# Values of the last two heads as a half slab behind the last queries and keys, and one plain loop of steps and products after it

## The chip, the cores and the metric

The kernel runs on one core of one Trainium2 chip. The metric is the device time of one execution in microseconds. In the text PE is TensorE, DVE is VectorE, ACT is ScalarE, POOL is GpSimd and SP is SyncE, as in the profile.

## The reference

Two decoder layers over 512 tokens of width 1024: a causal convolution module first, then differential attention; each is followed by a SwiGLU network and a gated input embedding. The change lies in the attention layer:

```
u = rms_norm(h, attn_norm_g)
q, k, v = split(u @ w_qkv)                    # 8 heads; each has two query/key halves of 64 and a value of 128
q, k = rms_norm per half
probs = softmax(q k^T + bias, causal)          # per head and half, in blocks of 128 queries
o = (probs[half 0] - lam * probs[half 1]) @ v
h = h + (rms_norm(o) * const) @ w_o
```

## The kernel before

Every large product is made as three products of TensorE (`mm3`, lines 162 to 166): each operand is split into a high and a low part, and low*high, high*low and high*high are added up in one PSUM bank. Weights come in tiles of 128x1024 through `weight` (lines 147 to 160): one DMA on SP's queue, a copy on ACT (L157, the high part) and a subtraction (L159, the low part) on VectorE, or on GpSimd where the caller asks for it. Raw tiles have two buffers, the split ones four.

**Queries, keys and values.** The table `QKV` (line 89) lists six slabs of w_qkv in order: queries and keys of a pair of heads ("q", 0 to 3) or values of four heads ("v", 0 and 1). A slab is 512 columns wide and takes four weight tiles (`slab`). For each of four blocks of 128 tokens, `tokens` multiplies eight chunks of the activations (stationary, 128x128) with the slab's columns (moving, 512 wide): 24 products. A value block is evicted by ACT (L867, high) and VectorE (L868, low) into the tile of that block. A query/key block is copied and squared by ACT (L884, L887), summed by VectorE (L891), its root is taken by GpSimd (L223) and applied by GpSimd (L894); `unit_end` then transposes it with four products (L900) into a "tp" bank and empties that with four ACT, four GpSimd and four VectorE operations (L908, L909, L913, L916, L918). There are two "tp" banks.

**Block steps.** Each of 32 blocks (head, 128 queries) has three stages. `stage_s` makes the scores (L945, L946), adds bias and takes the row limit (L948), the exponentials (L952) and the weighted difference of the two halves (L955 to L957). `stage_t` transposes it into a "tp" bank (L965) and splits it (L967 on ACT, L968 on VectorE). `stage_a` multiplies with the values (L981, L982); for odd blocks ACT and VectorE empty the bank (L988, L989), and after the last block of a head the head is normalised (L993 to L1003, POOL for L223 and L1003). The stages form one list of 96, in groups of (s of block n, t of block n-2, a of block n-3). `stage_o` transposes a finished head (L1010) into a "tp" bank and splits it (L178, L179).

**Order.** Up to the last slab, the compiler orders each engine's instructions by a planner with costs of its own. `QKV` holds, for each block of each slab, how many groups of three stages are put between its products: 21 groups in all, so 63 of 96 stages. `unit_end` of a block stands in the products of the next block. The last block of the last query/key slab has no next one; its `unit_end` is kept in `waiting`. From line 1102 on, TensorE's order is the written one: two groups of three products from `filling` (48 groups in all: 16 of the embedding projection, 32 of the first half of the output projection), then nine times (a stage, a group), then the kept `unit_end`, then (a stage, a group) while stages last. `step` also calls `stage_o` at every third count if a head is far enough. After the stages the rest of the groups run, with the last two `stage_o` between them, and then the second half of the output projection. Instructions that the planner placed can stand between the written ones.

Of the kernel before, what the change touches and what calls it, by code (L numbers as in the profile page):

```python
# [20 lines left out]
P = 128  # L21
# [52 lines left out]
LT = 2  # L74
AHEAD = 9
LA = 3
# [11 lines left out]
SEVEN = ((0,3),(1,0),(1,1),(1,2),(1,3),(2,0),(2,1),(2,2))  # L88
QKV = (("q", 0, (0, 0, 0, 0)), ("v", 0, (0, 1, 1, 0)), ("q", 1, (1, 1, 2, 2)), ("q", 2, (0, 1, 2, 0)), ("v", 1, (1, 2, 2, 2)), ("q", 3, (0, 2, 0, 1)))


@with_exitstack
def trunk(ctx, tc, xT, pT, wts, diag, dww, vec, rel, onehot, lamv, out):
# [744 lines left out]

    def slab(n=0):
        ws = [weight(eng=G if i < n else V) for i in range(4)]  # L840
        return [
            tuple(t[:, j * S : (j + 1) * S] for t in ws[k])
            for k in range(4)
            for j in range(2)
        ]

    def tokens(ws, tb, between=()):
        acc = mm()
        for k in range(NC):
# [10 lines left out]

    val = {}

    def values(s, ws, tb, between):
        acc, r = tokens(ws, tb, between)
        vt_ = sb([P, 4, 2, P], f"B{4 * s + tb}", 1, F32R)
        a3 = acc.rearrange("p (h d) -> p h d", h=4)
        A.activation(vt_[:, :, 0, :], a3, AF.Copy, scale=r)  # L867
        V.scalar_tensor_tensor(vt_[:, :, 1, :], a3, r, f(vt_[:, :, 0, :]), ALU.mult, ALU.subtract)  # L868
        for i in range(4):
            val[4 * s + i, tb] = vt_[:, i].rearrange("p a d -> p (a d)")  # L870

# [283 lines left out]
def _moving(w):  # L1155

    return w.reshape(4, 2, P, S).transpose(0, 2, 1, 3).reshape(4, P, 2 * S)

# [15 lines left out]
def _layout(a):  # L1174
# [26 lines left out]
    for what, at, _ in QKV:  # L1201
        if what == "v":
            slab = qkv[:, 2 * D + at * S : 2 * D + (at + 1) * S]
# [69 lines left out]
```

## Time and profile before

| | us |
|---|---|
| median of 3 runs | 1285.0 (1282.96 to 1287.46) |
| the profiled execution: its own time | 1287.74 |
| its span, first to last instruction | 1286.0 |
| PE busy in the span | 1253.1 (97%) |
| DVE busy in the span | 918.5 (71%) |
| ACT busy in the span | 615.5 (48%) |
| POOL busy in the span | 275.0 (21%) |

The attention layer's slabs and steps lie between 640 us and about 857 us of the span. The four value blocks of heads 4 to 7 are evicted by ACT at 742.9, 747.0, 754.6 and 760.9 us, the last query/key slab's products run from about 761 to 791.7 us, and the written order begins with the embedding projection's first product at 791.7 us. The stage list ends at 849.1 us with the last product of `stage_a`. A row of a timeline gives the start, the duration, the engine, the line, the operation, output and input tiles, shapes and count, and in brackets the idle time of the engine before it with what ended it. [...] A row of the stage table gives for each engine the busy time and in parentheses the instruction count, then the granted TensorE clock (1.00 is full) and the DMA share.

### The profile page before, as it was taken

The numbers are of one execution on the slowest core, as the hardware profiler recorded it, in microseconds if no ns is written. First come the engines' busy times: TensorE is split into PE (matmuls) and PEld (weight loads), VectorE is DVE, ScalarE is ACT, GpSimd is POOL, SyncE is SP. The second block draws the span as 40 slices with busy tenths as digits, with TensorE's granted clock in tenths as the row PEclk, the third lists the DMA queues.
The fourth block names the chain that finished last, engine by engine and source line by source line (L and its number), as shares of the span: only waits on it lengthen the run. The fifth ranks groups of instructions, "written<-read, shape, count | busy, mean of one in ns | idle before, by whom it ended". The sixth has DMA issues, their size and how long they took to land.

```text
span 1286.0 us, 18421 instructions
## 1 busy us (share of the span) xinstructions
PE 1253.1 (97%) x7056; PEld 1087.8 (85%) x7056; DVE 918.5 (71%) x1478; ACT 615.5 (48%) x1019; POOL 275.0 (21%) x239
## 2 busy tenths in 40 slices
PE   8999899999999999999999998899999999999998
PEld 5878678889899989988788887778888899899887
DVE  6988655785578557776678888866974588558665
ACT  5543355443255325454566768634642355225442
POOL 4645323000000000023335534114000001000030
PEclk8999989999999999999999999999999999999999
DMA  6655313275457545243222223222464466434241
GB/s 236 207 164 169 115 49 115 67 210 136 120 149 185 151 116 139 70 119 101 75 94 87 85 75 108 82 62 78 132 173 131 125 171 178 136 111 119 82 136 66
DMA packets 61764, 158.37 MB, mean 123 GB/s; under 512 B 6467, under 2 KB 11075, under 8 KB 61676
## 3 DMA queue, kind: packets, MB, share of 16 engines
q1 hardware_dynamic: 54944, 136.99, 33.3%
q0 software_dynamic: 4608, 16.78, 7.9%
q10 hardware_dynamic: 2124, 3.43, 0.9%
q8 instruction: 55, 0.90, 0.3%
q14 instruction: 33, 0.27, 0.1%
HBM read 151.91 MB, written 4.21 MB: 121 GB/s over the span
## 4 chain that ended last, share of the span: by engine, by line
PE 80%; DVE 10%; DMA 3%; issue 3%; ACT 2%; POOL 1%; SPq 1%; ACTq 0%; DVEq 0%; POOLq 0%
PE mm L165 21%; PE mm L164 21%; PE mm L166 21%; PE tp L166 2%; PE tp L165 2%; PE tp L164 2%; DVE wlo L159 2%; DVE sc L402 1%; PE sc L165 1%; PE sc L164 1%; PE sc L166 1%; POOL wk L390 1%; DVE A L179 1%; DMA po<-big 1%; DMA wraw<-in_wts 1%
## 5 line engine op out<-in xcount | busy, mean ns | idle before, releaser
L165 PE MATMUL mm<-A,whi 128*128 128x512 f32 (+1 forms) x896 | 309.9, 347 | 2.9 <-DVE A L179 1.5
L164 PE MATMUL mm<-A,wlo 128*128 128x512 f32 (+1 forms) x896 | 308.2, 349 | 1.5 <-ACT A L178 0.8
L166 PE MATMUL mm<-A,whi 128*128 128x512 f32 (+1 forms) x896 | 307.7, 344 | 0.0
L157 ACT CAST whi<-wraw 128x1024 fp32r<-128x1024 f32 (+2 forms) x142 | 142.9, 1012 | 235.6 <-PE mm L166 105.7
L159 DVE TENSOR_TENSOR wlo<-wraw,whi 128x1024 fp32r<-128x1024 f32 (+2 forms) x138 | 176.3, 1280 | 61.2 <-ACT whi L157 61.0
L165 PEld LDWEIGHTS mm<-A,whi 128*128 128x128 f32 x896 | 171.0, 191 | 26.7 <-DVE A L179 5.2
L164 PEld LDWEIGHTS mm<-A,wlo 128*128 128x128 f32 x896 | 170.8, 191 | 23.3 <-DVE wlo L159 1.7
L166 PEld LDWEIGHTS mm<-A,whi 128*128 128x128 f32 x896 | 171.0, 191 | 20.1 <-issue 0.7
L165 PE MATMUL mm<-B,whi 128*128 128x512 f32 x368 | 144.2, 393 | 0.0
L166 PE MATMUL mm<-B,whi 128*128 128x512 f32 x368 | 143.9, 392 | 0.0
L164 PE MATMUL mm<-B,wlo 128*128 128x512 f32 x368 | 143.1, 397 | 0.0
L651 POOL DMA_DIRECT2D C<-in_wts x32 | 28.2, 880 | 510.3 <-DVE h L762 179.7
L198 POOL TENSOR_TENSOR acc<-acc,wk 128x512 f32<-128x512 f32 x42 | 67.6, 1608 | 231.2 <-ACT wk L197 122.6
L166 PEld LDWEIGHTS mm<-B,whi 128*128 128x128 f32 x368 | 69.5, 189 | 15.3
L164 PEld LDWEIGHTS mm<-B,wlo 128*128 128x128 f32 x368 | 69.6, 189 | 14.1
L165 PEld LDWEIGHTS mm<-B,whi 128*128 128x128 f32 x368 | 69.6, 189 | 14.0
L762 DVE TENSOR_TENSOR h<-mm,h 128x512 f32<-128x512 f32 x48 | 33.0, 687 | 65.0 <-PE mm L166 64.8
L166 PE MATMUL mm<-whi,A 128*128 128x512 f32 x192 | 75.6, 395 | 0.0
L165 PE MATMUL mm<-wlo,A 128*128 128x512 f32 x192 | 75.1, 396 | 0.0
L164 PE MATMUL mm<-whi,A 128*128 128x512 f32 x192 | 74.8, 396 | 0.0
L223 POOL TENSOR_TENSOR r<-v,mhalf 128x8 f32<-128x8 f32 (+1 forms) x31 | 46.7, 1508 | 113.7 <-DVE v L221 91.4
L644 DVE TENSOR_TENSOR wlo<-wraw,whi 128x1024 fp32r<-128x1024 f32 x32 | 39.2, 1224 | 31.2 <-ACT whi L643 31.2
(281 smaller groups left out, 2706.0 us busy)
## 6 DMA issues: line engine op xcount, KB each, us to landing
wraw<-in_wts SPq DMA_DIRECT2D x162, 512.0 KB, 3.7
C<-in_wts SPq DMA_DIRECT2D x32, 512.0 KB, 4.4
C<-in_wts POOLq DMA_DIRECT2D x32, 512.0 KB, 6.0
bias<-in_wts SPq DMA_DIRECT2D x32, 256.0 KB, 3.8
wraw<-in_wts SPq DMA_DIRECT2D x16, 384.0 KB, 3.1
D<-in_diag SPq DMA_DIRECT2D x22, 256.0 KB, 4.2
C<-in_diag SPq DMA_DIRECT2D x16, 256.0 KB, 5.3
h<-in_xT SPq DMA_DIRECT2D x8, 256.0 KB, 5.2
```

Of the source, the lines that this page charges most:

```text
L157: A.copy(hi[:, cut], raw[:, cut])
L159: eng.tensor_tensor(lo[:, cut], raw[:, cut], f(hi[:, cut]), ALU.subtract)
L164: T.matmul(acc, al, bh, start=first, stop=False)
L165: T.matmul(acc, ah, bl, start=False, stop=False)
L166: return T.matmul(acc, ah, bh, start=False, stop=last)
L179: V.scalar_tensor_tensor(lo, src, scale, f(hi), ALU.mult, ALU.subtract)
L198: self.last = self.eng.tensor_tensor(self.acc, self.acc, sq, ALU.add)
L223: last_pow[0] = G.tensor_tensor(r[:, :n], v[:, :n], mhalf[:, :n], ALU.pow)
L390: G.tensor_tensor(pacc, pacc, pr, ALU.add)
L644: V.tensor_tensor(lo, raw, f(hi), ALU.subtract)
L651: nc.gpsimd.dma_start(q, wts[i + 2].rearrange("p (a s) -> p a s", a=2), accum_op=ALU.add)
L762: V.tensor_tensor(h[m], acc, h[m], ALU.add)
```

## The change

`QKV` splits the values of heads 4 to 7 into two slabs of 256 columns: heads 4 and 5 where all four were before, heads 6 and 7 behind the last query/key slab. A value entry is now (first head, number of heads). The paces give 22 groups, so 66 stages stand among the slabs' products and 30 behind them. The half slabs take two weight tiles each, and their order in the weights' array follows. Value slabs no longer give a subtraction to GpSimd. The loads of the embedding features move from the third block of the last query/key slab to the first block of the last value slab. The last `unit_end` now stands in the products of that first block; `AHEAD` and the separate call go.

```diff
-AHEAD = 9
-QKV = (("q", 0, (0, 0, 0, 0)), ("v", 0, (0, 1, 1, 0)), ("q", 1, (1, 1, 2, 2)), ("q", 2, (0, 1, 2, 0)), ("v", 1, (1, 2, 2, 2)), ("q", 3, (0, 2, 0, 1)))
+QKV = (("q", 0, (0, 0, 0, 0)), ("v", (0, 4), (0, 1, 1, 0)), ("q", 1, (1, 1, 2, 2)), ("q", 2, (0, 1, 2, 0)), 
+       ("v", (4, 2), (1, 1, 1, 1)), ("q", 3, (0, 2, 0, 1)), ("v", (6, 2), (1, 1, 1, 1)))
...
-    def slab(n=0):
-        ws = [weight(eng=G if i < n else V) for i in range(4)]
-        return [
-            tuple(t[:, j * S : (j + 1) * S] for t in ws[k])
-            for k in range(4)
-            for j in range(2)
-        ]
+    def slab(n, cols):
+        per = 1024 // cols
+        ws = [weight(eng=G if i < n else V) for i in range(NC // per)]
+        return [tuple(t[:, j * cols : (j + 1) * cols] for t in w) for w in ws for j in range(per)]
 
     def tokens(ws, tb, between=()):
-        acc = mm()
+        acc = mm()[:, : ws[0][0].shape[1]]
...
-    def values(s, ws, tb, between):
+    vtile = {}
+
+    def values(at, ws, tb, between):
         acc, r = tokens(ws, tb, between)
-        vt_ = sb([P, 4, 2, P], f"B{4 * s + tb}", 1, F32R)
-        a3 = acc.rearrange("p (h d) -> p h d", h=4)
+        h0, nh = at
+        if h0 % 4 == 0:
+            vtile[h0 // 4, tb] = sb([P, 4, 2, P], f"B{h0 + tb}", 1, F32R)
+        vt_ = vtile[h0 // 4, tb][:, h0 % 4 : h0 % 4 + nh]
+        a3 = acc.rearrange("p (h d) -> p h d", h=nh)
...
-        ws = slab(GLO if at > 0 else 0)
+        ws = slab(GLO if what == "q" and at > 0 else 0, P * at[1] if what == "v" else S)
         for tb in range(4):
-            if (what, at, tb) == ("q", 3, 2):
+            if (what, at, tb) == ("v", (6, 2), 0):
...
         for _ in range(2):
             next(fill)
-        for _ in range(AHEAD):
-            step()
-            next(fill)
-        unit_end(*waiting)
         while stages:
             step()
             next(fill, None)
```

More of the change, by code (lines that the diff above doesn't have):

```diff
@@ L1155, in _moving @@
 def _moving(w):
-    return w.reshape(4, 2, P, S).transpose(0, 2, 1, 3).reshape(4, P, 2 * S)
+    n = 1024 // w.shape[1]
+    return w.reshape(NC // n, n, P, w.shape[1]).transpose(0, 2, 1, 3).reshape(NC // n, P, 1024)
 def _onehot():
@@ L1202, in _layout @@
         if what == "v":
-            slab = qkv[:, 2 * D + at * S : 2 * D + (at + 1) * S]
+            slab = qkv[:, 2 * D + at[0] * P : 2 * D + sum(at) * P]
         else:
```

4 lines of the change are left out of this document (2 added, 2 removed).

## The prediction

> **What bounds the kernel now.** I read first the table of busy time by stage, cut where the values of heads 4 to 7 begin, where TensorE's written order begins and where the stage list ends:
>
> ```profile
> 735.40:791.70 56.30, 55.63 (x299) 47.66 (x298) 48.59 (x137) 39.67 (x96) 26.28 (x25) 1.00 0.28 85
> 791.70:849.10 57.40, 48.54 (x269) 40.18 (x268) 50.17 (x133) 39.69 (x91) 12.23 (x14) 0.94 0.26 88
> ```
>
> While the planner sets the order (735.4 to 791.7), PE is busy for 55.63 of 56.30 us and VectorE for 48.59: PE is the bound and VectorE has room. Behind 791.7 it is the other way round: PE stands still for 57.40 - 48.54 = 8.86 us, its clock averages 0.94, and VectorE is busy for 50.17 of 57.40. A finer cut shows where:
>
> ```profile
> 791.70:799.50 7.80, 4.83 (x27) 3.65 (x25) 7.61 (x15) 7.49 (x16) 1.73 (x4) 1.00 0.27 89
> 799.50:806.30 6.80, 5.28 (x16) 4.10 (x17) 6.46 (x18) 3.64 (x8) 3.07 (x3) 0.50 0.53 168
> 806.30:849.10 42.80, 38.44 (x227) 32.42 (x227) 36.09 (x103) 28.56 (x68) 7.42 (x8) 1.00 0.22 76
> 849.10:857.50 8.40, 6.27 (x33) 4.93 (x33) 5.75 (x11) 3.43 (x5) 2.05 (x2) 1.00 0.16 59
> 857.50:860.90 3.40, 3.40 (x10) 2.63 (x9) 0.73 (x1) 0.00 (x0) 0.00 (x0) 0.50 0.52 154
> ```
>
> In the first 14.6 us of the written order VectorE is 98% and 95% busy (7.61 + 6.46 of 14.60, 96%), and PE only 4.83 + 5.28 us, the latter at clock 0.50. The 42.8 us after that run with PE at 38.44 (90%) and VectorE at 36.09 (84%). PE's own timeline in the first stretch names three waits:
>
> ```profile
> 796.47 0.63 PE L900 MATMUL tp<-ident,big 128*128 128x128 f32 x4 [0.57 <-DVE C L918]
> 800.11 1.12 PE L1010 MATMUL tp<-ident,D 128*128 128x128 f32 x4 [3.01 <-DVE wtl L968]
> 803.42 0.66 PE L965 MATMUL tp<-ident,big 128*128 128x128 f32 x2 [0.92 <-DVE C L918]
> ```
>
> Transposes wait for a "tp" bank that VectorE has not emptied: 0.57, 3.01 and 0.92 us. VectorE's timeline shows what it does meanwhile:
>
> ```profile
> 796.36 1.23 DVE L1072 TENSOR_TENSOR wlo<-wraw,whi 128x1024 fp32r<-128x1024 f32 x1
> ...
> 799.77 0.28 DVE L968 TENSOR_TENSOR wtl<-tp,wth 128x128 fp32r<-128x128 f32 x1
> 799.97 1.21 DVE L1072 TENSOR_TENSOR wlo<-wraw,whi 128x1024 fp32r<-128x1024 f32 x1
> ...
> 802.78 0.49 DVE L918 SCALAR_TENSOR_TENSOR C<-tp,vec,C 64x256 fp32r<-64x256 f32 x1
> ```
>
> The bank that `stage_o` wants at 797 is freed by a 0.28 us subtraction (L968) at 799.77, behind a weight split of 1.23 us, a sum and a whole stage's row limits; the next one is freed at 803 by the last of four operations of a `unit_end`. So the place is set by VectorE's backlog when the written order begins, and part of that backlog is the evictions of `unit_end`, which the planner pushed behind 791.7:
>
> ```profile
> L918 DVE SCALAR_TENSOR_TENSOR C<-tp,vec,C 64x256 fp32r<-64x256 f32 x7 | 3.4, 485 | 0.1
> L916 DVE SCALAR_TENSOR_TENSOR C<-tp,lam,C 64x256 fp32r<-64x256 f32 x6 | 2.9, 484 | 0.7 <-ACT C L909 0.7
> ```
>
> Thirteen of these ran in the written part (three blocks of four, and one more), 13 x 0.484 = 6.3 us. What PE could do there at full clock is 48.54 less half of the 5.28 us at clock 0.50, so 45.9 us in 57.4: 11.5 us are lost.
>
> **The change part by part.** *The narrower value products.* Removed: 4 x 24 products of 512 columns; added: 8 x 24 of 256, each with a weight load of its own. Their price is the distance between starts:
>
> ```profile
> 640.00 0.39 PE L166 MATMUL mm<-whi,A 128*128 128x512 f32 x1
> ...
> 641.36 0.39 PE L166 MATMUL mm<-whi,A 128*128 128x512 f32 x1
> ```
>
> ```profile
> 299.98 0.28 PE L166 MATMUL sc<-C,whi 128*128 128x256 f32 x1
> ...
> 300.94 0.28 PE L165 MATMUL mm<-A,whi 128*128 128x256 f32 x1
> ```
>
> Six steps of 512 columns in 1.36 us are 0.227 us each, eight of 256 in 0.96 us are 0.120. So 96 x 0.227 = 21.8 us become 192 x 0.120 = 23.0: **+1.2 us** of PE, none of it hidden, since PE is the bound there.
>
> *Evictions and splits.* Four evictions of 512 columns become eight of 256:
>
> ```profile
> L868 DVE SCALAR_TENSOR_TENSOR B<-mm,rcol,B 128x512 fp32r<-128x512 f32 x8 | 6.0, 746 | 0.6 <-ACT B L867 0.5
> L957 DVE SCALAR_TENSOR_TENSOR big<-rb,st,big 128x256 f32<-128x256 f32 x8 | 3.9, 484 | 0.2
> L159 DVE TENSOR_TENSOR wlo<-wraw,whi 128x1024 fp32r<-128x1024 f32 x18 | 23.8, 1330 | 2.5 <-ACT whi L157 2.4
> ```
>
> No row has this eviction at 256 columns. It is between half of 746 ns (nothing added) and the 484 ns of the 256-wide operation of the same kind (2 x 0.484 - 0.746 = 0.22 more, four times 0.9 us), and not below nothing, since the same elements pass in twice the instructions; I take 0.9, the row with a duration of that size. One subtraction that GpSimd did comes to VectorE, 1.2 us in the undisturbed rows (L1072 above, 1.23). Together +2.1 us of VectorE, which costs nothing where VectorE has room and its full length where it has none. [...]
>
> *What moves ahead of the written order.* 66 stages in place of 63: the last stage of block 19, the first of block 23, the transpose of block 21. VectorE's part of them by rows (the six small operations of about 0.16 by L955):
>
> ```profile
> L948 DVE CUSTOM_DVE_ANT_0 rb<-sc,bias 128x512 f32<-128x512 f32 x8 | 5.5, 684 | 0.9 <-PE sc L946 0.9
> L957 DVE SCALAR_TENSOR_TENSOR big<-rb,st,big 128x512 f32<-128x512 f32 x8 | 6.0, 744 | 0.0
> L995 DVE TENSOR_REDUCE v<-wk 128x4 f32<-128x512 f32 x8 | 5.4, 679 | 0.1
> L968 DVE TENSOR_TENSOR wtl<-tp,wth 128x256 fp32r<-128x256 f32 x8 | 3.3, 418 | 0.0
> L989 DVE TENSOR_TENSOR D<-mm,D 128x256 f32<-128x256 f32 x16 | 6.7, 419 | 3.8 <-ACT D L988 3.7
> L955 DVE RECIPROCAL st<-st 128x1 f32<-128x1 f32 x32 | 5.1, 158 | 3.7 <-ACT rb L952 2.3 <-ACT acc L952 1.0
> ```
>
> Block 23: 2 x 0.684 + 0.744 + two small ones 0.3 = 2.4; block 21: 0.42; block 19: 0.42 + 0.68 + five small ones 0.8 = 1.9. That is 4.7 us of VectorE and, at 512 columns per 0.227 us (block 23 four times 512 columns, block 19 four times 384, block 21 two times 128), 1.7 us of PE. The evictions of `unit_end` move too, since the last query/key block now has four value blocks and twelve stages behind it: 6.3 us of VectorE, 0.7 of PE (three blocks, 512 columns of transposes each), and with them one sum of squares:
>
> ```profile
> L891 DVE TENSOR_REDUCE v<-wk 128x8 f32<-128x512 f32 x13 | 8.8, 680 | 3.3 <-ACT wk L887 3.1
> L1098 DVE TENSOR_TENSOR h<-mm,h 128x512 f32<-128x512 f32 x6 | 4.1, 686 | 1.7 <-PE mm L166 1.7
> ```
>
> The written part has three steps fewer, and with them three groups of products (3 x 3 x 0.227 = 2.05 us of PE) and one L1098 run behind the stage list in place of before its end. The stage list may thus end at 849.1 - 2.05 = 847.05 without any gain; against that I count.
>
> *Sum.* Ahead of the written order: PE 55.63 + 1.2 + 1.7 + 0.7 = 59.2 us of work, at the share it has now (55.63 of 56.30) 59.9 us. VectorE has 48.59 + 2.1 + 4.7 + 6.3 + 0.7 = 62.4 us for it; at the 96% of its fullest stretch it does 57.7 of them and leaves 4.7 as backlog. In the written part: PE 45.9 - 2.4 - 2.05 = 41.45 us, at the 90% of the 42.8 us stretch 46.1; VectorE 50.17 - 4.7 - 6.3 - 0.7 - 0.7 = 37.8, and at 96% it could do 44.4, so 6.6 are free for the backlog. If all of it fits in, the list ends at 735.4 + 59.9 + 46.1 = 841.4, a gain of 5.6 us; if all of it is paid, at 846.1, a gain of 0.9. PE waits for single operations, not for sums, so I take half: **-3.3 us**.
>
> *What stays.* Behind the list the last `stage_o` waits for GpSimd's scaling of the last head as before:
>
> ```profile
> 856.06 0.66 PE L1010 MATMUL tp<-ident,D 128*128 128x128 f32 x4 [2.13 <-POOL D L1003]
> ```
>
> The written order calls it after the same number of groups behind the last stage, so 2.13 us and the half clock of 857.5 to 860.9 stay; three more groups follow. In the list four waits of `stage_s` for the row limit of its other half (4.2 us in all, the longest 1.6) also stay, since block 24 and all later ones start there as before:
>
> ```profile
> PE sc L945 <- DVE st L948: 4.2, 4, 1.6
> ```
>
> SP's queue has the same bytes in another order; the last query/key slab's later tiles now wait for the value slab's two tiles, and PE's cover is the first four chunks, 12 x 0.227 = 2.7 us, against 1.05 + 1.23 of copy and split; if VectorE is late, this is the next wait. The copy is this row's, the split L1072's above:
>
> ```profile
> L157 ACT CAST whi<-wraw 128x1024 fp32r<-128x1024 f32 x21 | 21.8, 1051 | 5.6 <-DMA wraw<-in_wts 2.7 <-PE mm L166 2.0 <-POOL r L223 0.8
> ```
>
> The second half of a value tile is written while the first is read; that makes no wait if parts of a tile are tracked apart, and the trace shows it:
>
> ```profile
> 816.55 0.34 PE L945 MATMUL sc<-C,C 128*128 128x384 f32 x1
> ```
>
> ```profile
> 818.58 0.49 DVE L918 SCALAR_TENSOR_TENSOR C<-tp,vec,C 64x256 fp32r<-64x256 f32 x1
> ```
>
> Those scores read blocks 0 to 2 of a key tile while the eviction of block 3 into it ran until 819.
>
> The profiled execution took 1287.74 us, 1.74 more than its span and 2.74 above the median. 1287.74 - 3.3 = 1284.4 for such an execution; from the median, 1285.0 - 3.3 = **1281.7 us**.
>
> **The rivals.** *The backlog fits in whole.* PE loses little anywhere, as in the planner's part now. Gain 5.6, and up to 9 if the 10% lost in the 42.8 us stretch also shrinks by 3.5 us. For it: VectorE's 84% there; against it: the `stage_s` waits stay. 1276 to 1279.4.
>
> *VectorE becomes the bound of the slabs (slower).* The three last slabs have 62.4 us of VectorE for 59.2 of PE. In the planner's part VectorE now works at 48.59 of 56.30, 86%. If it can't be fuller, since its operations wait for ACT and PE in turn, this part takes 62.4 / 0.863 = 72.3 us, and the list ends at 735.4 + 72.3 + 46.1 = 853.8, 6.8 us late. It decides at the share where 62.4 / x + 46.1 is 847.05 - 735.4: 95%. Against it: PE always has value or key products there that wait for nothing, and VectorE's 86% was PE's limit, not its own; so only a part of it would be paid. 1285 to 1292.
>
> *A new gap brings the half clock.* The rows above show clock 0.50 from 799.5, in the 3.01 us gap, for 6.8 us, and for 3.4 us behind one of 2.13. A new gap of 2 to 3 us in the half slabs or at the first `stage_o` would cost itself and half of 3.4 to 6.8 us, 3.8 to 6.4 in all: 1285.7 to 1288.3. [...]
>
> *It does nothing.* The planner can push the stages back behind the slab as it did with `unit_end`. 1284 to 1286.
>
> **How the numbers follow.** 0.3%, 3.9 us, is about what a measurement here can tell from no change: 1281.1 to 1288.9 is the same. Forecast (1280 to 1284) 0.46, of which 0.15 faster by over 0.3%; whole backlog absorbed 0.26, all faster; VectorE bound 0.17, of which 0.13 slower; new gap 0.05, of which 0.02 slower; nothing 0.06. So faster 0.41, same 0.44, slower 0.15. The range from 1275.5 to 1288.5 leaves out the far ends of both sides.
>
> **What would show it.** Right: no wait above 1 us of a transpose for a "tp" bank in the first 15 us of the written order, full clock there, VectorE's busy share over the half slab behind the last keys above 90%, PE's products there 0.12 us apart, and the 2.13 us wait and its half clock unchanged at the end. Wrong: PE idle for more than 3 us within the last two slabs, or the first `stage_o` again behind a weight split.

## The result and the profile after

| | before | after |
|---|---|---|
| median of 5 runs each, side by side, us | 1285.5 (1283.0 to 1287.5) | 1292.9 (1291.0 to 1295.5) |
| ratio, 95% interval | | 1.0061 (1.0043 to 1.0079) |
| the profiled execution: its own time / its span, us | 1287.74 / 1286.0 | 1292.92 / 1291.1 |

The change makes the kernel slower by 0.61%, some 7.4 us, where 3.3 us less had been forecast; the result lies outside the range. In the attention layer the lines of the kernel after are one higher than before (L946 for L945, L1073 for L1072). Its first slab product starts 2.0 us earlier than in the trace of before (616.14 against 618.16), from differences ahead of anything that the change touches, so the cuts that were at 735.4, 791.7 and 849.1 us are here at 733.3, 797.4 and 850.9. The first cut is not where the values of heads 4 to 7 begin: their first product starts at 729.12 in the trace of before and at 727.14 here. Up to the cut both kernels have made the same part of them, 18 products of 512 columns or 36 of 256, and the same stages, so the comparison from there on holds.

The stage table of the kernel after, cut at the same three places (the third row goes on to the last `stage_o`):

```profile
733.30:797.40 64.10, 61.14 (x388) 54.31 (x387) 52.16 (x149) 43.95 (x108) 29.92 (x32) 0.97 0.25 74
797.40:850.90 53.50, 46.23 (x250) 38.70 (x248) 42.43 (x126) 33.44 (x79) 6.14 (x6) 0.90 0.29 94
850.90:859.50 8.60, 5.33 (x29) 4.16 (x28) 4.59 (x10) 2.64 (x4) 2.05 (x2) 1.00 0.19 61
```

The planner's part takes 64.1 us where it took 56.3 (+7.8), the written part 53.5 where it took 57.4 (-3.9). From the end of the list to the last `stage_o` it is 859.16 - 850.9 = 8.26 us, and was 856.06 - 849.1 = 6.96 (+1.3); the three groups of products that now run behind it are another 2.05. That makes 7.8 - 3.9 + 1.3 + 2.05 = 7.25 us, all of the loss. PE's busy time in the written part, at full clock, is what was forecast: 46.23 less half of the 7.99 us in the half-clock row below is 42.2, against 41.45. So PE's work moved much as the prediction said, and most of the time was lost in waits and clock. Sorted by kind, PE stands still for 1.8 us more (2.3 more in the planner's part and 1.1 at the end, 1.6 less in the written part). The half clock costs 3.1 us more: half of the 3.40, 7.99 and 3.41 us that PE was busy in it here, against half of 5.28 and 3.40 before. Half is an estimate from the granted 0.50: in the kernel after, products of 512 columns start 0.426 us apart from 751.27 to 754.25 and 0.226 apart at full clock, from 754.66 to 756.24. About 2.3 us are more work, of which the narrow products, priced below, are 1.7. A finer cut, with the half clock behind the last wait as its last row:

```profile
733.30:746.80 13.50, 12.98 (x101) 11.95 (x99) 13.08 (x39) 9.96 (x27) 9.74 (x10) 1.00 0.22 75
746.80:751.20 4.40, 2.07 (x11) 1.50 (x11) 4.37 (x11) 4.32 (x10) 1.84 (x2) 1.00 0.47 131
751.20:754.60 3.40, 3.40 (x9) 2.65 (x9) 3.29 (x12) 1.57 (x7) 0.04 (x1) 0.50 0.75 210
754.60:780.00 25.40, 25.40 (x133) 21.50 (x132) 14.77 (x45) 14.28 (x34) 9.22 (x11) 1.00 0.02 6
780.00:797.40 17.40, 17.29 (x140) 16.70 (x139) 16.66 (x47) 13.82 (x34) 9.07 (x10) 1.00 0.46 132
...
802.40:812.60 10.20, 7.99 (x26) 6.54 (x27) 8.18 (x27) 4.63 (x12) 2.05 (x2) 0.50 0.42 129
...
860.43:863.84 3.41, 3.41 (x10) 2.64 (x9) 1.44 (x2) 0.88 (x2) 0.00 (x0) 0.50 0.00 0
```

VectorE, the third busy time of a row, is full in the first half slab behind the cut (13.08 of 13.50 us, then 4.37 of 4.40 and 3.29 of 3.40) and in the second (16.66 of 17.40, 96%), and has room in the query/key slab between them (14.77 of 25.40, 58%). In the first half slab PE stands still while VectorE is full. The granted clock is 0.50 for 3.4 us behind that gap, and for 10.2 us (6.8 before) in the written part, where it falls at 802.40, ahead of the longest wait there. PE's timeline names the waits:

```profile
745.79 0.30 PE L966 MATMUL tp<-ident,big 128*128 128x128 f32 x1 [0.32 <-DVE st L957]
...
749.16 0.39 PE L946 MATMUL sc<-C,C 128*128 128x256 f32 x1 [2.09 <-DVE st L949]
749.90 0.33 PE L946 MATMUL sc<-C,C 128*128 128x128 f32 x1 [0.24 <-DVE st L949]
...
804.75 0.48 PE L983 MATMUL mm<-B,wtl 128*128 128x128 f32 x1 [1.82 <-DVE wtl L969]
...
859.16 0.66 PE L1011 MATMUL tp<-ident,D 128*128 128x128 f32 x4 [3.27 <-POOL D L1004]
```

And VectorE's timeline shows what stands ahead of each releaser, the operation that ended the wait:

```profile
746.75 1.22 DVE L159 TENSOR_TENSOR wlo<-wraw,whi 128x1024 fp32r<-128x1024 f32 x1
747.89 0.21 DVE L957 SCALAR_TENSOR_TENSOR st<-st,lam 128x1 f32<-128x1 f32 x1
748.02 0.48 DVE L869 SCALAR_TENSOR_TENSOR B<-mm,rcol,B 128x256 fp32r<-128x256 f32 x1
748.41 0.68 DVE L949 CUSTOM_DVE_ANT_0 rb<-sc,bias 128x512 f32<-128x512 f32 x1
...
803.27 1.22 DVE L1073 TENSOR_TENSOR wlo<-wraw,whi 128x1024 fp32r<-128x1024 f32 x1
804.41 0.28 DVE L969 TENSOR_TENSOR wtl<-tp,wth 128x128 fp32r<-128x128 f32 x1
...
853.13 1.23 DVE L1073 TENSOR_TENSOR wlo<-wraw,whi 128x1024 fp32r<-128x1024 f32 x1 [0.40 <-ACT whi L1072]
854.27 0.68 DVE L996 TENSOR_REDUCE v<-wk 128x4 f32<-128x512 f32 x1
```

It is one picture three times. In the half slab the scores wait for a bank that the row limit of 748.41 empties, behind a weight split and an eviction of values. At the start of the written order `stage_a` waits for the subtraction at 804.41, behind a split of output weights. At the end the last head's sum of squares at 854.27 stands behind a third split (and its squares, on ACT from 853.00, behind the copy of the same weights at 852.04), and the last `stage_o` waits 3.27 us in place of 2.13. The waits of the scores alone are 7.0 us in eight over the whole execution, where they were 4.2 in four; one of 1.6 us lies ahead of the values of heads 4 to 7 in both:

```profile
PE sc L946 <- DVE st L949: 7.0, 8, 2.1
```

### The profile page after: what moved, and what is told of

Read it like the earlier page. It is cut to its first block, busy times and chain, and to the rows that moved or that the text cites. A ratio compares the mean times of both kernels' runs of the same rounds, so it can differ in the third digit from the quotient of the medians.

```text
span 1291.1 us, 18622 instructions
## 1 busy us (share of the span) xinstructions
PE 1256.1 (97%) x7152; PEld 1093.8 (85%) x7152; DVE 912.7 (71%) x1483; ACT 615.2 (48%) x1023; POOL 271.1 (21%) x238
## 4 chain that ended last, share of the span: by engine, by line
PE 79%; DVE 10%; DMA 4%; issue 3%; ACT 2%; POOL 1%; SPq 0%; DVEq 0%; POOLq 0%; ACTq 0%
PE mm L165 22%; PE mm L164 21%; PE mm L166 21%; PE tp L166 2%; PE tp L165 2%; PE tp L164 2%; DVE wlo L159 2%; PE sc L165 1%; PE sc L164 1%; PE sc L166 1%; DVE sc L402 1%; POOL wk L390 1%; DMA C<-in_wts 1%; DVE A L179 1%; DMA po<-big 1%
## 5 line engine op out<-in xcount | busy, mean ns | idle before, releaser
L166 PEld LDWEIGHTS mm<-B,whi 128*128 128x128 f32 x368 | 69.5, 189 | 15.3
L166 PE MATMUL mm<-whi,A 128*128 128x512 f32 (+1 forms) x224 | 81.8, 366 | 0.0
L165 PE MATMUL mm<-wlo,A 128*128 128x512 f32 (+1 forms) x224 | 81.5, 366 | 0.0
L164 PE MATMUL mm<-whi,A 128*128 128x512 f32 (+1 forms) x224 | 81.3, 369 | 0.0
```

The costliest lines, as they stand in the source:

```text
L164: T.matmul(acc, al, bh, start=first, stop=False)
L165: T.matmul(acc, ah, bl, start=False, stop=False)
L166: return T.matmul(acc, ah, bh, start=False, stop=last)
```

## The experiments

All were timed in five rounds beside the kernel before on the same chip; a ratio is to that kernel, with its 95% interval (its medians beside them were 1284.5 to 1285.8 us). The last column is from each kernel's one trace, from attention's first slab product to the last product of the program: it leaves out the spread of what lies ahead (that first product came between 612.5 and 618.2 us). It is one execution each, and the verdicts go by the ratios.

| kernel | median us | ratio (interval) | attention on, us |
|---|---|---|---|
| before | | 1 | 662.8 |
| after | 1292.9 | 1.0061 (1.0043 to 1.0079) | 670.0 |
| spread | 1287.9 | 1.0020 (1.0007 to 1.0032) | 666.8 |
| later | 1291.6 | 1.0046 (1.0030 to 1.0061) | 670.0 |
| even | 1285.5 | 1.0007 (0.9997 to 1.0017) | 661.7 |
| inplace | 1291.4 | 1.0042 (1.0026 to 1.0058) | 668.4 |
| inplace2 | 1292.0 | 1.0045 (1.0029 to 1.0061) | 670.3 |
| held | 1293.6 | 1.0067 (1.0047 to 1.0088) | 670.6 |
| held2 | 1287.1 | 1.0011 (0.9994 to 1.0028) | 668.1 |
| before_held2 | 1285.4 | 0.9999 (0.9982 to 1.0017) | 665.1 |
| spread_held2 | 1286.4 | 1.0007 (0.9993 to 1.0021) | 665.0 |
| twice | 1286.5 | 1.0006 (0.9986 to 1.0026) | 665.1 |
| evict | 1285.5 | 0.9998 (0.9980 to 1.0015) | 661.8 |
| vonly | 1281.9 | 0.9977 (0.9959 to 0.9994) | 658.8 |
| pool2 | 1294.1 | 1.0063 (1.0040 to 1.0086) | 670.5 |
| after_vonly | 1290.2 | 1.0038 (1.0023 to 1.0054) | 667.4 |
| inplace2_vonly | 1284.4 | 0.9996 (0.9982 to 1.0010) | 662.5 |
| before_held2_vonly | 1283.4 | 0.9983 (0.9965 to 1.0002) | 658.0 |
| spread_held2_vonly | 1283.4 | 0.9981 (0.9964 to 0.9998) | 660.4 |
| even_vonly | 1285.6 | 1.0006 (0.9995 to 1.0018) | 660.0 |

### The parts that were priced: narrow products and cut evictions

`twice` is the kernel before with each product of the values of heads 4 to 7 made as two of 256 columns; `evict` is that kernel with only the evictions of these values cut in two.

```diff
-            mm3(acc, a, ws[k], k == 0, k == NC - 1)
+            mm3(acc[:, cut], a, tuple(t[:, cut] for t in ws[k]), k == 0, k == NC - 1)   # twice: all k of one half, then of the other
...
+        for i in (slice(0, 2), slice(2, 4)) if s else (slice(0, 4),):                    # evict: L867 and L868 once for each i
```

> The kernel before with each product of the values of heads 4 to 7 made as two of 256 columns, one half after the other into the same bank, and one eviction as before. Theory B1 (the narrow products cost the loss by themselves): 1289 to 1292. Theory A: their price is the distance between starts, 192 x 0.1225 - 96 x 0.2275 = 1.7 us, 1286.5 to 1287.5.

> The kernel before with each of the four evictions of the values of heads 4 to 7 cut in two (ScalarE and VectorE, 256 columns each), products as before. Theory B2 (VectorE is so full between 735 and 760 us that 0.9 us more of it opens a wait and a half clock): 1288 to 1291. Theory A: 0.9 us that the products beside it hide for the most part, 1285 to 1286.5.

Measured: +0.06% and -0.02%, neither to be told from nothing; the medians differ by 1286.5 - 1285.0 = 1.5 us for `twice`. The rows of the kernel after agree with that size. Sixteen steps of narrow products there, from 738.21 to 740.17, are 1.96 / 16 = 0.1225 us each from start to start (a row is 0.28 to 0.34 us long, so the rows overlap), so 192 of them take 23.5 us and 1.7 more than the 21.8 before; the two rows are the first and the last of the sixteen, and the transpose behind them starts at 740.17:

```profile
738.21 0.34 PE L166 MATMUL mm<-whi,A 128*128 128x256 f32 x1
...
740.05 0.28 PE L166 MATMUL mm<-whi,A 128*128 128x256 f32 x1
```

The eight narrow evictions take 474 ns each where four wide ones, those of heads 0 to 3 in the same trace, took 750, 3.8 - 3.0 = 0.8 us of VectorE:

```profile
L869 DVE SCALAR_TENSOR_TENSOR B<-mm,rcol,B 128x256 fp32r<-128x256 f32 x8 | 3.8, 474 | 0.0
L869 DVE SCALAR_TENSOR_TENSOR B<-mm,rcol,B 128x512 fp32r<-128x512 f32 x4 | 3.0, 750 | 0.6 <-ACT B L868 0.5
```

So neither part, alone and in a slab of the old shape, makes the loss; the interval of `twice` leaves room for 0.26% at most.

### The pace of the half slabs

`spread`, `later` and `even` are the kernel after with other paces, in groups of three stages for each block of tokens.

```diff
-("v", (4, 2), (1, 1, 1, 1)), ("q", 3, (0, 2, 0, 1)), ("v", (6, 2), (1, 1, 1, 1))   # after
+("v", (4, 2), (0, 1, 0, 1)), ("q", 3, (1, 2, 1, 1)), ("v", (6, 2), (1, 1, 1, 1))   # spread
+("v", (4, 2), (1, 1, 1, 1)), ("q", 3, (0, 2, 0, 1)), ("v", (6, 2), (0, 1, 0, 1))   # later
+("v", (4, 2), (0, 1, 1, 1)), ("q", 3, (1, 1, 1, 1)), ("v", (6, 2), (0, 1, 1, 1))   # even
```

> The changed kernel with six of the twelve stages of the first half slab moved to the last query/key slab (paces 0,1,0,1 and 1,2,1,1 in place of 1,1,1,1 and 0,2,0,1). Theory A (VectorE and ScalarE are oversubscribed while twelve stages stand in 11.5 us of half-slab products, so PE waits about 2.9 us there and loses 1.7 to the half clock): both go, 3.5 to 4.5 us below the changed kernel, 1288 to 1289.5. Theory B (the narrow products and evictions cost it by themselves): no change, 1292 to 1294. Theory C (the new place behind the keys and the new written order cost it): no change, 1292 to 1294.

> The changed kernel with six of the twelve stages of the last half slab left to the written order (paces 0,1,0,1). Theory A: VectorE comes to the written order with less backlog, the waits of about 3.5 us and the half clock of 10 us in its first 15 us shrink to under half, 3 to 5 us below the changed kernel, 1288 to 1290; the stall at the first half slab stays. Theory B: no change, 1292 to 1294. Theory C: no change or, with two more steps' groups in the written order, 1 to 3 slower.

> The kernel after with three stages in each half slab and four in the third query/key slab, instead of four, three and four: as many stages ahead of the written order as in the kernel before, and at no place more to the microsecond than its seven in 23 us. Theory P with D (the loss is lumps on a full VectorE, with GpSimd's held operation as a second cause): the half slabs' stalls (2.86 us in the kernel after) and their half clock go down to some 1 us, one VectorE split at the start of the written order remains in the way, and with the narrow products' 1.5 us the time is 1286.5 to 1288.5. Rival N (the three stages taken ahead were the useful part of the change; without them the written order is longer by what the slabs are shorter and the waits at its start stay): 1290 to 1293, as in the kernel after.

`spread` has as many stages ahead of the written order as the kernel after, two groups of them moved from the first half slab to the query/key slab behind it, and wins back two thirds of the loss (1.0061 to 1.0020). `later` takes two groups out of the second half slab and wins back nothing that the intervals separate. `even` takes one group out of each and gives one to the slab between, and nothing of the loss is left that can be told from zero.

In the trace of `spread`, the row from the first product of the values of heads 4 and 5 to the first product of the written order shows no idle time of PE and full clock:

```profile
725.14:788.17 63.03, 63.03 (x431) 58.05 (x429) 56.52 (x156) 47.16 (x112) 32.33 (x33) 1.00 0.27 80
```

The kernel after takes 70.3 us for it. Part of that comes back in the written part of `spread`, where PE stands still for 9.1 us (7.27 in the kernel after) and the half clock lasts 13.65 us (10.24).

In the trace of `even`, the row of the stage table for the first half slab, from about the same cut on:

```profile
732.90:749.60 16.70, 16.33 (x113) 14.85 (x111) 16.14 (x44) 13.04 (x32) 10.93 (x12) 1.00 0.27 87
```

and PE's waits behind it:

```profile
749.63 0.39 PE L946 MATMUL sc<-C,C 128*128 128x256 f32 x1 [0.40 <-DVE st L949]
751.16 0.50 PE L165 MATMUL mm<-wlo,A 128*128 128x512 f32 x1 [1.03 <-DVE wlo L159]
```

VectorE is as full as in the kernel after (16.14 of 16.70, 97%), but PE waits 0.40 and 1.03 us instead of 0.32, 2.09 and 0.24, and the clock stays at 1.00. So a full VectorE alone is not what costs. The reading that fits these orders, argued and not tested by itself, is that the group of stages more costs because it stands ahead of the releaser that PE waits for when no slab product is left in front of that wait. Nor do the three stages more ahead of the written order bring anything that shows: `even` has none of them.

The trace of `even` does not win its time in the slabs as a whole. From the first product of the values to the first of the written order it takes 69.5 us, against 70.3 in the kernel after, since another wait comes at the end of the last half slab. It wins behind them: 50.9 us of written part against 53.5, and a last wait of 2.11 us with full clock behind it against 3.27 us with half clock. Every kernel here with 66 stages ahead of the written order has that last wait at 3.26 to 3.28 us.

The longest wait that `even` and `spread` have left lies around the start of the written order, whose first product runs at 796.24 in `even` and at 788.17 in `spread`. In `even`, ACT's timeline and PE's:

```profile
792.05 1.04 ACT L1072 CAST whi<-wraw 128x1024 fp32r<-128x1024 f32 x1 [2.68 <-DMA wraw<-in_wts]
```

```profile
795.86 0.58 PE L982 MATMUL mm<-B,wth 128*128 128x256 f32 x1 [3.78 <-ACT wth L968]
```

ACT waits 2.68 us for the DMA of the first output weights, with their copy at the head of its queue, and the exponentials and the split that PE waits for stand behind it. In `spread` it is the same, 1.30 us of the copy and 3.57 of PE, there at 795.19.

### The split of the output weights at the start of the written order

`held` puts VectorE's split of each tile of the first half of the output weights behind the split of the third-last block that `stage_t` has transposed so far, and those of the second half behind the last; `held2` holds ACT's copy in the same way too, and takes the fourth-last block for the first half; `before_held2` does so in the kernel before, and `spread_held2` in `spread`.

```diff
+        back = -4 if first == 0 else -1
+        with tc.issue_after(tcopy[back].ins):     # held: without this, and -3
             A.copy(hi, raw)
+        with tc.issue_after(tsplit[back].ins):
             V.tensor_tensor(lo, raw, f(hi), ALU.subtract)
```

> The changed kernel with VectorE's splits of the first half of the output weights held behind the split of the third last transposed block, so that two of 1.22 us each no longer stand in the first stretch of the written order. Theory A (backlog on VectorE): 2.4 us less in front of the transposes, PE's wait of 1.8 us goes and the half clock behind it is shorter, 3 to 5 us below the changed kernel, 1288 to 1290. Theories B and C: no change, 1292 to 1294.

> The changed kernel with both ScalarE's copy and VectorE's split of the first output weights held behind those of the fourth last transposed block. Theory A2 (in the first 15 us of the written order these weights stand in front of the blocks' evictions in both queues, ScalarE's copy waiting for its DMA): waits there under 1 us in sum and no half clock, 3 to 5 us below the changed kernel, 1288 to 1290. Rival (the backlog of the blocks themselves): no change, 1292 to 1294.

> The kernel before with the same holding of the first output weights. Theory A2: its waits of 3.6 and 0.9 us and the 6.8 us of half clock at the start of the written order shrink to under half, 1279 to 1282. Rival (the evictions of the transposes and the blocks' own backlog): no change, 1285 to 1287.

> The changed kernel with the sparser first half slab (0,1,0,1 and 1,2,1,1) and the holding of the first output weights. Theory A with A2: both stalls gone, 1280 to 1283, faster than the kernel before. Rival (the blocks' own backlog at the written order's start): 1287 to 1289 as without the holding.

`held` moves the stall and cures nothing. In its trace, ACT's copy of a later pair of weights, VectorE's split and PE's wait:

```profile
823.67 1.05 ACT L1075 CAST whi<-wraw 128x1024 fp32r<-128x1024 f32 x1 [1.47 <-DMA wraw<-in_wts]
```

```profile
827.43 1.21 DVE L1076 TENSOR_TENSOR wlo<-wraw,whi 128x1024 fp32r<-128x1024 f32 x1
```

```profile
829.38 0.58 PE L946 MATMUL sc<-C,C 128*128 128x256 f32 x1 [3.43 <-DVE st L949]
```

`held2`, with ACT's copy held as well, is 1.0011, and in its trace, whose lines are two higher, the 1.82 us wait of `stage_a` is 0.42. The stall of the first half slab stands in it unchanged:

```profile
746.08 0.58 PE L946 MATMUL sc<-C,C 128*128 128x256 f32 x1 [2.09 <-DVE st L949]
...
800.33 0.47 PE L985 MATMUL mm<-B,wtl 128*128 128x128 f32 x1 [0.42 <-DVE wtl L971]
```

So by the ratios this hold alone gives back most of the loss too; its one trace shows less of it, 668.1 us against 670.0 from attention on. Both cures together, `spread_held2`, are at 1.0007: not the sum of 0.41 and 0.50%, but about where each of them ends, and no interval separates the three. That both waits are one backlog of VectorE, which drains as soon as either place lets it, would fit the ratios, but the traces do not show it: `spread` loses the first stall and waits longer at the start of the written order, and `held2` shortens the second and keeps the first. Why the two cures do not add stays open. The same hold in the kernel before moves nothing (0.9999): its waits of 3.01 and 0.92 us at the start of the written order become 1.27 and 1.44, and others grow behind them, such as the last one, from 2.13 to 3.29 us.

### The half slabs in the old place

`inplace` is the kernel before with the two half slabs one behind the other where the whole one was, at its pace, its written order kept; `inplace2` moves one group of stages from the first half to the second, so that the stages lie no denser than in the kernel before. GpSimd does one subtraction of the first half slab, as it did of the whole one.

```diff
-("v", 1, (1, 2, 2, 2)), ("q", 3, (0, 2, 0, 1))
+("v", (4, 2), (1, 1, 1, 1)), ("v", (6, 2), (1, 1, 0, 1)), ("q", 3, (0, 2, 0, 1))   # inplace
+("v", (4, 2), (0, 1, 1, 1)), ("v", (6, 2), (1, 1, 1, 1)), ("q", 3, (0, 2, 0, 1))   # inplace2
```

> The kernel before with the values of heads 4 to 7 as two half slabs one behind the other in the old place, with the old 21 groups of stages (1,1,1,1 and 1,1,0,1), the old nine steps ahead of the last transposes, and one subtraction on GpSimd as before. Theory B: most of the loss is here, 1290 to 1293. Theories A and C: only the narrow products, 1.2 to 1.7 us of PE and 0.9 of VectorE, 1286.5 to 1288.

> As the two half slabs in the old place, but with the stages no denser than in the kernel before: paces 0,1,1,1 and 1,1,1,1 put 1, 3, 5 and 7 groups behind each quarter of the values, as 1,2,2,2 did. Theory A (the dense stages of the first half slab): no wait above 1 us there, 1286.5 to 1288.5, that is the narrow products alone. Theory B (narrow products and evictions by themselves): 1290 to 1293, as with the denser paces.

Both lose about as much as the kernel after, 0.42 and 0.45%, and against the theory of the pace: `inplace2` has no more stages anywhere than the kernel before. The range of the theory of the narrow products came true, but `twice` and `evict` have shown that these do not make it. In its trace, VectorE, GpSimd and PE:

```profile
741.09 2.56 DVE L958 SCALAR_TENSOR_TENSOR big<-rb,st,big 128x256 f32<-128x256 f32 x1
```

```profile
740.97 2.38 POOL L159 TENSOR_TENSOR wlo<-wraw,whi 128x1024 fp32r<-128x1024 f32 x1
```

```profile
746.89 0.33 PE L946 MATMUL sc<-C,C 128*128 128x128 f32 x1 [2.69 <-DVE st L949]
749.60 0.45 PE L966 MATMUL tp<-ident,big 128*128 128x128 f32 x1 [1.60 <-DVE C L919]
```

An operation that takes 484 ns elsewhere took 2.56 us, and it ends at 743.65 just behind GpSimd's subtraction (743.35). That made a new theory: GpSimd's share of the splits costs VectorE as much as it saves.

### GpSimd's share of the splits

`GLO` is the number of subtractions of a slab that GpSimd does: 1 in both kernels, 0 in `vonly` and in every `_vonly`, 2 in `pool2`.

```diff
-GLO = 1
+GLO = 0
```

> The kernel before with all weight splits of the slabs on VectorE (four of 2.4 us leave GpSimd). Theory D (while GpSimd splits a tile, VectorE's own operation stands: 2.35 and 2.56 us in place of 0.2 and 0.48 in the traces): VectorE gains 2 us and pays 1.2 for each, no change or 1 to 3 faster, 1282 to 1286. Rival (the two engines work side by side): 4 x 1.2 us more on a VectorE that is over 86% busy, 1287 to 1290.

> The kernel before with two of four weight splits of the slabs on GpSimd in place of one. Theory D: each takes 2 us from VectorE to save it 1.2, 1286 to 1290. Rival: VectorE is relieved by 4 x 1.2 us, 1281 to 1284.

> The two half slabs one behind the other in the old place, no stage denser than before, and GpSimd's share of the splits set to none. Theory D: of the 6.5 us by which this layout lies above the kernel before, narrow products make 1.5 and cut evictions 0; the held operation of 2.56 us at 741.09 and the gaps of 2.69 and 1.60 us with their half clock of 6.8 us make the rest, and they go: 1281.9 (the kernel before without GpSimd's share) plus 1.5 to 2.5 is 1283.4 to 1284.4, so it is below the kernel before by 0 to 0.15%. Rival W (a half slab has 48 products of 0.12 us, so its weights and its split must come in half the time, and VectorE's six subtractions for it stand in the way of the stages whoever else splits): the gaps stay, 1289 to 1292.

> The kernel after, with GpSimd's share of the slab splits set to none: the one split of each query/key slab that GpSimd still makes goes to VectorE (three more subtractions of 1.24 us on VectorE, three of 2.39 us fewer on GpSimd). Theory D (while GpSimd subtracts, a VectorE operation is held for up to 2 us, and so the split costs VectorE as much there as here): in the kernel before, four such splits given back brought 3.1 us (1281.9 against 1285.0), so three bring 2 to 3.5 us here, 1289.4 to 1291; if the held operation of 2.02 us at the head of the last query/key slab is what makes the half slab's stall of 2.09 us at full VectorE, that stall and its 3.4 us of half clock go as well, and the time is 1287 to 1289. Rival P (the loss comes from the lumps of the pace alone; GpSimd's share lightens VectorE): VectorE gets 3.7 us more work where it is 96 to 99% busy, and the time is 1293 to 1296.

> The kernel after with the first half slab at two stages' pace and the third query/key slab at five, the first output weights' split held behind the fourth-last stage_t, and GpSimd's share of the splits set to none. With GpSimd's share it took 1286.4 against 1285.4 for before. Theory D: three splits given back bring 2 to 3.5 us, 1283 to 1284.5, so at last below the kernel before, and about 1 to 2 us above that kernel without GpSimd's share, for the narrow products. Rival L (taken together the change has something to give: three stages and the evictions of the last query/key slab lie ahead of the written order, and once VectorE is not held and not loaded in lumps the 3.3 us that were predicted come): 1278 to 1280.5, below the kernel before without GpSimd's share. Rival P (GpSimd's share lightens VectorE): 1287 to 1290.

> The kernel before with GpSimd's share of the slab splits set to none, and the split of the first output weights held behind the fourth-last stage_t. Each alone: 1281.9 against 1285.0, and 1285.4 against 1285.4. Theory B (the backlog that meets the written order is paid there or later, whatever its order on VectorE): the holding moves only the place of the waits, and the time is that without GpSimd's share, 1281 to 1283. Rival H (with VectorE lightened by 2.5 us ahead of it, the held split finds room, and the 3.4 us gap and the 6.8 us of half clock at the start of the written order go): 1276 to 1279.

> The same with GpSimd's share of the slab splits set to none. Theory P with D: 1281.9 (the kernel before without GpSimd's share) plus the narrow products' 1.5 us, 1282.5 to 1284.5; the stall in the half slab that stayed in the kernel after without GpSimd's share (1.68 us, 6.8 us of half clock) is gone. Rival N: 1287 to 1290, like that kernel's 1290.2 or little better. Rival L (with VectorE neither held nor loaded in lumps, the value slab's evictions of the last query/key slab lie ahead of the written order, and its start is free): 1278 to 1281, below the kernel before without GpSimd's share.

None, one and two in the kernel before give 0.9977, 1 and 1.0063. In the trace of before, an operation of VectorE on 128x4 takes 2.35 us while GpSimd subtracts from 724.95 to 727.34:

```profile
725.02 2.35 DVE L221 TENSOR_SCALAR v<-v 128x4 f32<-128x4 f32 x1 [0.31 <-POOL r L223]
```

```profile
724.95 2.39 POOL L159 TENSOR_TENSOR wlo<-wraw,whi 128x1024 fp32r<-128x1024 f32 x1
```

In `vonly` the same operation takes 0.17:

```profile
722.95 0.17 DVE L221 TENSOR_SCALAR v<-v 128x4 f32<-128x4 f32 x1
```

And in `pool2` two of VectorE's are held beside two of GpSimd's in a row: the first takes 2.86 us where it usually takes 0.74, and the second ends at 763.50, where GpSimd ends (758.29 + 5.20 = 763.49):

```profile
758.38 2.86 DVE L957 SCALAR_TENSOR_TENSOR big<-rb,st,big 128x512 f32<-128x512 f32 x1
761.35 2.15 DVE L956 SCALAR_TENSOR_TENSOR st<-st,lam 128x1 f32<-128x1 f32 x1
```

```profile
758.29 5.20 POOL L159 TENSOR_TENSOR wlo<-wraw,whi 128x1024 fp32r<-128x1024 f32 x2 [3.10 <-issue]
```

In these rows the slow operation of VectorE ends with GpSimd's, at 727.37 against 727.34 and at 763.50 against 763.49; what ties the two engines together was not shown.

`inplace2_vonly` decides what the half slabs in the old place lost: 1.0045 becomes 0.9996, as expected (1283.4 to 1284.4, measured 1284.35). Of PE's waits of 2.69 and 1.60 us one of 1.03 is left (the wait of 4.0 us at the start of the written order, which both have, stays):

```profile
749.07 0.33 PE L946 MATMUL sc<-C,C 128*128 128x128 f32 x1 [1.03 <-DVE st L949]
```

In the kernel after the same edit brings less, 1.0061 to 1.0038, which the intervals do not separate, and the stall of the first half slab stays (1.68 us, with 6.8 us of half clock); `spread` brought more there, so the pace is the larger cause; the second half of that expectation, that the stall would go with the held operation, fell. `spread_held2_vonly` is at 0.9981, in the range of that theory and not of the one that hoped for the predicted gain. `before_held2_vonly` is not better than `vonly`. `even_vonly` is no faster than `even` (1.0006 and 1.0007), against its expectation; its one trace is 1.6 us shorter, 4.1 us in the slabs, of which the written part gives 2.5 back, and why GpSimd's share costs nothing there is not settled.

The fastest kernel of all is `vonly`, the kernel before with GpSimd out of these splits: 0.9977 (0.9959 to 0.9994) of the kernel before. No kernel with the half slabs, in either place, came out below it, though `spread_held2_vonly` (0.9981) cannot be told from it.

## Why the prediction was wrong

**The work was sized right.** The narrow products cost 1.7 us of PE (forecast 1.2), the cut evictions 0.8 us of VectorE (0.9), the three groups behind the list 2.05, and PE's work in the written part is 42.2 us (41.45). Together these miss by about a microsecond.

**Where the forecast missed.** The planner's part took 4.2 us more than forecast (64.1 against 59.9), the written part 5.0 us more (53.5 against 46.1 and half of the 4.7 us of backlog), and the last wait 1.1 us more.

**The step that failed is the sum of VectorE's work over the whole of the planner's part**, "at the 96% of its fullest stretch it does 57.7 of them and leaves 4.7 as backlog", and behind it "PE waits for single operations, not for sums, so I take half". The part was to take 59.9 us and took 64.1. VectorE did not work in it at 96% but at 52.16 of 64.10, 81%: full in both half slabs, 58% in the slab between, since the paces put twelve stages in each half slab and nine in the query/key slab, which is nearly twice as long in products. In the kernel before, VectorE had room in both of its slabs there, 29.40 of 32.18 us (91%) in the values and 25.00 of 30.40 (82%) in the queries and keys:

```profile
729.12:761.30 32.18, 31.51 (x170) 26.83 (x169) 29.40 (x80) 24.78 (x61) 16.95 (x18) 1.00 0.29 83
761.30:791.70 30.40, 30.40 (x166) 26.11 (x165) 25.00 (x73) 21.10 (x49) 12.34 (x12) 1.00 0.34 109
```

Room in the middle was of no use to work that was due ahead of it or behind it. `spread` shows it most plainly: with two groups moved into that room the same 66 stages pass without idle time of PE. Of the 7.8 us by which the part grew, 2.4 are the moved work, 1.4 the narrow products (156 of the 192 lie behind the cut), 2.3 more idle time of PE (64.10 - 61.14 = 2.96 against 0.67) and 1.7 the half clock (half of 3.40).

**The rival that came true was given 0.17 and turned down with a wrong sentence**: "PE always has value or key products there that wait for nothing". From 744.28 to 750.55 us no slab product runs on PE: the half slab's own are done, and the next slab's stand behind the scores of 749.16 in PE's order. A product that waits for nothing did not help behind scores that waited 2.09 us. The rival's size was also too small (1285 to 1292), since it had only VectorE's share in it and not the clock. The rival of the new gap, given 0.05, has the right size for the first half slab: a gap of about 2 us and half of 3.4 us of half clock. Both came at once, with a third wait besides.

**The start of the written order did not come free.** The forecast took its waits as part of the backlog that the moved evictions of `unit_end` had made; nine of the thirteen did move (four are left behind 797.4), and the last half slab's own stages and last eviction (802.28) took their place beside two splits of output weights at 801.07 and 803.27, which stood there before too. So the written part is 3.9 us shorter, though 4.45 us of PE's work left it (2.4 and 2.05). The forecast had 7.0 us of loss in it (46.1 - 41.45 and half of 4.7), with full clock; 11.3 came (53.5 - 42.2), 7.3 of them idle time, 1.6 less than before, and 4.0 from 10.2 us of half clock. `held2` shows that copies and splits of output weights have a part in it. The forecast also put four waits of the scores (4.2 us) into this part; three of them, 2.6 us, lie there.

**"so 2.13 us and the half clock of 857.5 to 860.9 stay"**: the half clock did, but the wait is 3.27 us. The groups were counted and the splits between them were not; a split at 853.13 now runs ahead of the last head's sum of squares.

**"One subtraction that GpSimd did comes to VectorE, 1.2 us"** has the wrong sign by the runs without GpSimd's share: the rows of before with 2.35 us for an operation of 0.17 stood in the trace and were read past. This did not make the loss of the change, but it is the largest gain that the runs found.

**The signs named ahead.** Right as forecast: products 0.12 us apart, VectorE above 90% in the last half slab, no wait above 1 us for a "tp" bank early in the written order. Wrong: full clock there, and the unchanged 2.13 us. Neither sign for failure showed. PE was idle for 0.1 us in the last two slabs; the stall lay in the first half slab (2.85 us), which the sign left out. The first `stage_o`, at 807.81, did not wait; `stage_a` stood behind the weight split in its place.

**What stays open.** With even paces the change is worth nothing (1.0007), about what `twice` alone is (1.0006); that its gain is just eaten by the narrow products is the likely reading and was not tested. The two traces, from the first product of the values on, fit it: in `even` PE has 1.7 us more work than in the kernel before and 1.3 us less idle time; it also has 1.6 us less loss by the half clock, which came behind the last wait in one (2.13 us) and not in the other (2.11 us). Why `held2` helps the kernel after and not the kernel before, and why GpSimd's share costs 0.16 to 0.49% in five layouts (clear of the intervals in `vonly` and `inplace2_vonly` alone) and nothing in `even`, is not settled.

## What to carry to other kernels

Before moving work to an engine with room on average, draw its busy share slab by slab at the pace that the change sets, and look at the in-order queue in front of each wait: two groups of stages placed otherwise, out of the first half slab or one out of each, won back 5 to 7 us here, with room for them in the slab between. A gap of 2 us is priced with the half clock that can come with it (3.4 us of it behind the gap of 2.09 us here), and two cures that each win back most of a loss need not add. An operation that takes many times its usual length beside another engine's (2.35 us for one of 0.17 here) is worth an experiment of its own before anything is moved.

## What the runs showed of the hardware

Beside a subtraction of 128x1024 on GpSimd (2.39 us in the kernel before, 2.38 in `inplace2`) an operation of VectorE lasted until that one's end or 0.3 us longer: 2.35 us for one of 0.17 (to 727.37, GpSimd to 727.34), 2.56 for one of 0.48 (to 743.65, GpSimd to 743.35). On VectorE the same subtraction took 1.23 us (L1072 in the kernel before), so the share that was to lighten it held it for 2.2 and 2.1 us to spare it 1.2. Not every operation was held. During another of them in the kernel before, from 756.89 to 759.31,

```profile
756.89 2.42 POOL L159 TENSOR_TENSOR wlo<-wraw,whi 128x1024 fp32r<-128x1024 f32 x1 [2.88 <-issue]
```

```profile
757.32 0.69 DVE L995 TENSOR_REDUCE v<-wk 128x4 f32<-128x512 f32 x1
758.16 0.29 DVE L948 CUSTOM_DVE_ANT_0 acc<-sc,bias 128x128 f32<-128x128 f32 x1 [0.15 <-PE sc L946]
758.37 0.08 DVE L948 DVE_READ_ACCUMULATOR2_ANT st<- 128x1 f32 x1
758.37 0.96 DVE L998 TENSOR_TENSOR v<-v,r 128x4 f32<-128x4 f32 x1
```

a sum and a row limit ran at the length that they have elsewhere in that trace (0.69 us, and 0.68 at 723.24; 0.29 us, and 0.27 at 738.48), and only the small product of L998 was held, until 759.33: 0.96 us, and 0.15 at 724.37. So such a subtraction cost VectorE 2.2 us at 725 and 0.8 here; what decides which operation is held was not tested.

In the attention layer the half clock came in lengths of 6.83 and 3.41 us in the kernel before, of 3.41, 10.24 and 3.41 in the kernel after and of 13.65 in the written part of `spread`, one to four times 3.41. In the traces of before and after its beginnings lie whole multiples of 3.41 us apart too: 799.46 and 857.48 us before, 17 times, and 751.21, 802.41 and 860.43 us after, 15 and 17 times. The length of a gap alone did not settle whether it came. In the kernel after, 3.4 us of it began 2.05 us behind the end of a gap of 2.09 us, and three waits of 0.67, 0.33 and 0.29 us stood ahead of the 10.24 us that began at 802.41. Behind a gap of 2.72 us in `before_held2_vonly` none came, here with the clock of its stretch, 1.00; whether it matters when a gap begins was not tested:

```profile
848.62 0.66 PE L1012 MATMUL tp<-ident,D 128*128 128x128 f32 x4 [2.72 <-POOL D L1005]
```

```profile
840.00:860.00 20.00, 17.28 (x84) 14.18 (x83) 11.52 (x16) 5.20 (x7) 2.98 (x3) 1.00 0.33 105
```
